# A decoder layer on one core: the merging of two attentions is spread over more steps, with hi and lo rows in one operand

## Chip, core and metric

The kernel runs on one core of a Trainium2 chip. The metric is device time in microseconds (us) of one execution. Three runs of the kernel before gave 892.7, 892.76 and 892.86 us; the median is 892.76.

The engines are named as the profile names them: PE multiplies matrices (PEld loads its stationary operand), DVE and ACT work element by element, POOL is a further such engine, SP issues most of the DMAs. Each engine takes its instructions in the order in which the program lists them.

## What is computed

One decoder layer of width 1024 over 512 tokens: a projection, two mixers side by side (dilated attention, and a state space model with a gated linear unit), their gated sum, a norm, and a gated feed-forward with a second norm. The change concerns the end of the attention, where the outputs of three dilation groups are merged by their softmax denominators:

```python
for g, (window, dilation) in enumerate(DILATION_GROUPS):   # (128,1), (512,4), (2048,16)
    o_g, lse_g = dilated_group_attention(q[:, :, g], k[:, :, g], v[:, :, g], window, dilation)
    outs.append(o_g)
    lses.append(lse_g)
wts = jax.nn.softmax(jnp.stack(lses, axis=0), axis=0)
attn = jnp.sum(wts[..., None] * jnp.stack(outs, axis=0), axis=0)
y_attn = attn.reshape(bsz, s, ATTN_WIDTH).astype(x.dtype) @ w_attn_br[layer]
...
glu = jax.nn.gelu(y_s).astype(x.dtype) @ w_glu[layer]
y_s = glu[..., :SSM_WIDTH] * jax.nn.sigmoid(glu[..., SSM_WIDTH:])
y_ssm = y_s @ w_ssm_br[layer]
```

## The kernel before

Every fp32 operand of a large product is held as two parts, hi and lo (`split`: ACT rounds the hi part, DVE subtracts to get the lo part), and a product is three matmuls, hi by hi, hi by lo and lo by hi (`mm3`, L186 to L188). A tile of 512 tokens by 128 channels is a chain of such triples into one PSUM bank. Weights come by DMA in units of 1 MB and are split likewise, one half at each `w.release()`: ACT writes `whi`, DVE writes `wlo`.

The order is written out by hand. The program is a list of steps, one PE tile or pair of tiles each, and `at_step(n, fn)` hangs smaller work into step n: a whole number runs in the middle of the step (`mid`, after half of the matmuls, or where a later loop calls `run_fill`), a number ending in .5 at its end. Steps 0 to 55 are the tiles of the first projection; 52 to 55 are gate tiles (`pg`). Steps 56 to 59 are the four tile pairs of the gated linear unit (GLU, banks `gl`, in a ring of four banks, so pair n+2 overwrites pair n). Its eviction is a tanh on ACT (`th`), a multiply on DVE, and a split into `gh` and `gl`. Steps 60 to 63 multiply its result by the state space branch's weights (banks `b`), steps 64 to 67 do the same for the attention's result (`ath`, `atl`).

The attention itself runs between these tiles. It is done in two kinds: kind 0, near, is the first dilation group; kind 1, far, is the other two together. Each unit of work has scores (PE, `s`), a masked maximum (DVE) and an exponential (ACT), transposes of the result into a bank (`t`, PE; there are two such banks, `turned`, taken in turn), a copy of that bank by ACT (`tv`), and the values (PE, `o`). Far attention's units are at steps 46 to 56.5; near attention is done by step 40.5. Each kind leaves its outputs in `oa` and two statistics per head and token in `st`: a shifted maximum and a sum.

The merge then needs, per head and token, the weight of each kind. Before the change:

- Step 56, after the matmuls of the first GLU pair and ahead of its eviction: `merge_stats` loads the selector `sel` (8 rows, one per head; it spreads a head's weight over its 64 channels), turns the statistics of both kinds with 16 transposes through the two `turned` banks (`stb`), copies them by DVE, takes the common maximum, and exponentiates on ACT.
- Step 57, ahead of the second pair's eviction: `merge_weights`, three operations of DVE and a reciprocal.
- Step 58, ahead of the third pair's eviction: `merge_split` makes hi and lo parts (`whl`) of the two weights, each of 8 rows, as four separate operands.
- Steps 59.5 to 62.5: `merge_pair`, for each pair of heads, spreads the weights by four matmuls (`wb`, two per kind, hi and lo added in PSUM) and scales and adds the two outputs on DVE; ACT and DVE split the sum.

In the profile the small helpers have one line for all callers: `split` is L179, L180, L182 and L183, `tt` is L302, `stt` is L299.

Of the kernel before, what the change touches and what calls it, by code (L numbers as in the profile page):

```python
# [10 lines left out]
F32 = mybir.dt.float32  # L11
# [3 lines left out]
ALU = mybir.AluOpType  # L15
# [39 lines left out]
def by_phase(z):  # L55
    return z.rearrange("p (r h c) -> p r h c", r=4, h=2)
# [96 lines left out]
def emit(ctx, tc, i, out):  # L153
# [48 lines left out]
    def big(n, name, dt=F32):  # L202
        return pa.tile([P, 2048], dt, tag=f"big{n}", name=name)
# [574 lines left out]

    merged = {}

    def merge_stats():
        sel = at.tile([8, NPAIR, P], F32, tag="sw", name="sel")
        sp.dma_start(sel, i["sel"])
        stt_ = big(1, "sts")
        sts = [[stt_[0:8, 512 * (2 * k + e) : 512 * (2 * k + e + 1)] for e in range(2)] for k in range(2)]
        for kind in range(2):
            for e in range(2):
                b = turned(f"stb{kind}{e}")
                for blk in range(4):
                    pe.transpose(b[0:8, 128 * blk : 128 * blk + 128], st[kind][:, e, blk, :], ident)  # L790
                if kind == 0:
                    dve.tensor_copy(by_phase(sts[kind][e]), as_phases(b[0:8]))
                else:
                    dve.tensor_copy(sts[kind][e], b[0:8])
        mg = at.tile([8, 512], F32, tag="sw", name="mg")
        tt(mg, sts[0][0], sts[1][0], ALU.min)
        for kind in range(2):
            tt(sts[kind][0], mg, sts[kind][0], ALU.subtract)
        for kind in range(2):
            act.activation(sts[kind][0], sts[kind][0], AF.Exp)  # L800
        merged.update(sel=sel, sts=sts)

    def merge_weights():
        sts = merged["sts"]
        zg = at.tile([8, 512], F32, tag="cq", name="zg")
        for kind in range(2):
            tt(sts[kind][1], sts[kind][0], sts[kind][1], ALU.mult)
        tt(zg, sts[0][1], sts[1][1], ALU.add)
        dve.reciprocal(zg, zg)
        merged["z"] = zg  # L810

    def merge_split():
        sts = merged["sts"]
        selr = at.tile([8, NPAIR, P], F32R, tag="tv", name="selr")
        dve.tensor_copy(selr, merged["sel"])
        hl = big(3, "whl", F32R)
        whl = [[hl[0:8, 512 * (2 * k + e) : 512 * (2 * k + e + 1)] for e in range(2)] for k in range(2)]
        for kind in range(2):
            tt(sts[kind][0], sts[kind][0], merged["z"], ALU.mult)
        for kind in range(2):  # L820
            act.copy(whl[kind][0], sts[kind][0])
        for kind in range(2):
            tt(whl[kind][1], sts[kind][0], whl[kind][0].bitcast(F32), ALU.subtract)
        merged.update(sel=selr, w=whl)
        for j, n in (("g1", "h"), (1, "l")):
            merged[n] = home(j, f"at{n}", F32R).rearrange("p (q t) -> p q t", q=4)

    def merge_pair(hp):
        wb = [turned(f"wb{hp}{k}") for k in range(2)]
        for kind in range(2):  # L830
            for e in range(2):
                pe.matmul(wb[kind], merged["sel"][:, hp, :], merged["w"][kind][e], start=(e == 0), stop=(e == 1))
# [130 lines left out]
    for n in range(4):  # L963
        ws = w.views[N_GLU + n]
        bs = []
        for e in range(2):
            b = glu(f"gl{n}{e}")
            co = slice(128 * e, 128 * e + 128)
            for k in range(4):
                mm3(b, (ws[0][:, k, co], ws[1][:, k, co]), (gluin["y"][0][:, k, :], gluin["y"][1][:, k, :]), k == 0, k == 3)  # L970
            bs.append(b)
        run_fill(N_GLU + n)
        th = at.tile([P, 512], F32, tag="sw", name=f"th{n}")
        act.activation(th, bs[1], AF.Tanh, scale=0.5)
# [232 lines left out]
def constants():  # L1207
# [18 lines left out]
    sel = np.zeros((8, NPAIR, P), f32)  # L1226
    for hp in range(NPAIR):
        for m in range(P):
            sel[2 * hp + m // 64, hp, m] = 1.0
    return {"rope": rope, "masks": masks, "sel": sel, "ident": np.eye(P, dtype=f32)}  # L1230


# [72 lines left out]
```

## Time and profile before

| what | value |
|---|---|
| median of three runs | 892.76 us |
| the profiled execution, whole | 892.44 us |
| its span in the trace | 890.7 us |
| steps 56 to 59, first GLU matmul to first matmul of step 60 | 390.65 to 419.03 us |
| steps 60 to 63, to the first matmul on `ath` | 419.03 to 447.33 us |
| granted TensorE clock, mean | 0.997 |

The page gives each engine's busy time. A timeline row gives start and duration in us, engine, line, operation and the tiles it writes and reads; `x8` means that eight neighbours are merged into a row; in brackets at its end stands how long the engine was idle before it, and what it waited for. Matmuls overlap in the trace, so two starts, not a duration, give PE's pace.

### The profile page before, as it was taken

The page shows a single profiled execution, that of the slowest core. Times are in us where ns is not written, and L with a number is a line of the kernel's source. Part 1 is how long each engine was busy: PE and PEld are TensorE (multiplying, and loading weights), DVE is VectorE, ACT ScalarE, POOL GpSimd, SP SyncE. Part 2 cuts the span into 40 slices and gives each one's busy share as a digit, 9 for nine tenths or more (in the row PEclk, how much of TensorE's full clock was granted, in tenths as well). Part 3 has the DMA queues.
Part 4 walks back from the last instruction along what each step waited for, and adds up shares of the span by engine and source line. Part 5 has one row for each costly group of instructions (what it writes and reads, how often), then busy time and mean ns, then how long its engine had stood idle before and what let it go on. Part 6 is the DMA issues. An engine that isn't in the chain of part 4 may idle for free.

```text
span 890.7 us, 11572 instructions
## 1 busy us (share of the span) xinstructions
PE 874.8 (98%) x4710; PEld 725.8 (81%) x4710; DVE 487.1 (55%) x929; ACT 292.2 (33%) x474; POOL 25.1 (3%) x26
## 2 busy tenths in 40 slices
PE   8999999999999999999999999999999999999996
PEld 5888888888878988876788898888888888888885
DVE  7887876665365464347876765333444444322237
ACT  5353521234442234544234233222222222211101
POOL 0000000000000000000000310000000000000004
PEclk9999999999999999999999999999999999999998
DMA  8843798062122222111225414222222222322203
GB/s 312 186 111 108 187 141 191 4 186 95 54 89 81 71 88 82 61 50 53 100 84 214 164 49 142 94 95 95 95 95 95 95 95 95 141 95 95 95 0 95
DMA packets 34789, 95.27 MB, mean 107 GB/s; under 512 B 11560, under 2 KB 21544, under 8 KB 25520
## 3 DMA queue, kind: packets, MB, share of 16 engines
q1 hardware_dynamic: 33152, 91.92, 33.6%
q10 hardware_dynamic: 1584, 2.61, 0.8%
q8 instruction: 37, 0.61, 0.3%
q14 instruction: 16, 0.13, 0.1%
HBM read 86.43 MB, written 4.69 MB: 102 GB/s over the span
## 4 chain that ended last, share of the span: by engine, by line
PE 49%; issue 40%; DVE 5%; DMA 3%; ACT 2%; POOL 2%; SPq 0%; DVEq 0%; POOLq 0%
PE pg L186 3%; PE pg L187 3%; PE pg L188 3%; PE pv L186 3%; PE pv L188 3%; PE pv L187 3%; PE pq L186 2%; PE pq L188 2%; PE pq L187 2%; PE pk L186 2%; PE s L733 2%; PE pk L188 2%; PE pk L187 2%; PE t L757 2%; PE b L186 2%
## 5 line engine op out<-in xcount | busy, mean ns | idle before, releaser
L180 DVE TENSOR_TENSOR wlo<-raw,whi 128x1024 fp32r<-128x1024 f32 x136 | 166.4, 1227 | 202.0 <-ACT whi L179 201.8
L179 ACT CAST whi<-raw 128x1024 fp32r<-128x1024 f32 x136 | 141.8, 1047 | 205.7 <-PE dn L188 74.8
L186 PE MATMUL fg<-hh,whi 128*128 128x512 f32 (+1 forms) x384 | 143.5, 374 | 0.0
L188 PE MATMUL fg<-hh,wlo 128*128 128x512 f32 (+1 forms) x384 | 143.4, 373 | 0.0
L187 PE MATMUL fg<-hl,whi 128*128 128x512 f32 (+1 forms) x384 | 143.4, 373 | 0.0
L187 PEld LDWEIGHTS fg<-hl,whi 128*128 128x128 f32 x384 | 72.3, 188 | 13.4
L188 PEld LDWEIGHTS fg<-hh,wlo 128*128 128x128 f32 x384 | 72.3, 188 | 13.3
L186 PEld LDWEIGHTS fg<-hh,whi 128*128 128x128 f32 x384 | 72.3, 188 | 13.3
L186 PE MATMUL dn<-whi,ff 128*128 128x512 f32 x168 | 66.0, 393 | 0.0
L188 PE MATMUL dn<-whi,ff 128*128 128x512 f32 x168 | 65.9, 392 | 0.0
L187 PE MATMUL dn<-wlo,ff 128*128 128x512 f32 x168 | 65.8, 392 | 0.0
L186 PE MATMUL pg<-x_hi,whi 128*128 128x512 f32 x128 | 50.6, 395 | 0.0
L188 PE MATMUL pg<-x_hi,wlo 128*128 128x512 f32 x128 | 49.9, 390 | 0.0
L187 PE MATMUL pg<-x_lo,whi 128*128 128x512 f32 x128 | 49.8, 389 | 0.0
L182 ACT ACTIVATE ff<-fth 128x512 fp32r<-128x512 f32 x22 | 13.9, 634 | 101.6 <-DVE fth L302 101.6
L745 ACT ACTIVATE pt<-pt,st 128x256 f32<-128x256 f32 (+1 forms) x64 | 31.0, 485 | 45.2 <-DVE st L743 45.2
L302 DVE TENSOR_TENSOR fth<-fth,fg 128x512 f32<-128x512 f32 x22 | 15.1, 688 | 55.8 <-PE fg L188 55.6
L186 PE MATMUL pq<-x_hi,whi 128*128 128x512 f32 x96 | 38.1, 397 | 0.0
L186 PE MATMUL pk<-x_hi,whi 128*128 128x512 f32 x96 | 38.0, 396 | 0.0
L188 PEld LDWEIGHTS dn<-whi,ff 128*128 128x128 f32 x168 | 31.5, 188 | 7.3
L188 PE MATMUL pq<-x_hi,wlo 128*128 128x512 f32 x96 | 37.4, 390 | 0.0
L188 PE MATMUL pk<-x_hi,wlo 128*128 128x512 f32 x96 | 37.4, 390 | 0.0
(236 smaller groups left out, 1592.0 us busy)
## 6 DMA issues: line engine op xcount, KB each, us to landing
raw<-in_w_in SPq DMA_DIRECT2D x27, 1024.0 KB, 5.1
raw<-in_w_gu SPq DMA_DIRECT2D x22, 1024.0 KB, 4.7
raw<-in_w_dn SPq DMA_DIRECT2D x11, 1024.0 KB, 4.7
raw<-in_w_br SPq DMA_DIRECT2D x4, 1024.0 KB, 4.8
raw<-in_w_out SPq DMA_DIRECT2D x4, 1024.0 KB, 4.7
cas<-ca SPq DMA_DIRECT2D x8, 256.0 KB, 7.8
tm<-kdr SPq DMA_DIRECT2D x16, 128.0 KB, 8.7
raw<-in_w_glu SPq DMA_DIRECT2D x2, 1024.0 KB, 4.7
```

What stands on the lines that cost most here:

```text
L179: act.copy(hi, src)
L180: dve.tensor_tensor(lo, src, hi.bitcast(F32), op=ALU.subtract)
L182: act.mul(hi, src, scale)
L186: pe.matmul(dst, a[0], b[0], start=first, stop=False)
L187: pe.matmul(dst, a[0], b[1], start=False, stop=False)
L188: pe.matmul(dst, a[1], b[0], start=False, stop=last)
L302: eng.tensor_tensor(o, a, b, op=op)
L733: pe.matmul(banks[hh][:, 256 * j + 128 * c : 256 * j + 128 * (c + nk)], z[0][rows, hp, qs], z[1][rows, hp, 128 * k0 : 128 * (k0 + nk)], st ...
L745: act.activation(pt[:, :n], pt[:, :n], AF.Exp, bias=mneg, scale=-1.0, accum_out=zsum)
L757: pe.transpose(tb[:, hh, cs], pts[hh][:, cs], ident)
```

## The change

Statistics are turned one kind at a time: the near ones in the middle of step 52, the far ones at the end of step 55. The further work of the merge is cut into smaller pieces, `merge_shift` (56.5), `merge_sum` (57.5), `merge_reciprocal` (58) and `merge_split` (59). In the GLU's loop `run_fill(N_GLU + n)` moves behind the eviction and the release of the weights. The pairs move from 59.5 + hp to 60 + hp, the middle of steps 60 to 63. Hi and lo rows of a weight become one operand of 40 rows, hi in rows 0 to 7, lo in rows 32 to 39, zeros between (filled by POOL), and the selector has its rows twice, so that one matmul per kind and pair does both. The small tiles of the merge now lie in the table `rope`, whose last reader is step 51, and in one scratch tile.

```diff
-    def merge_stats():
-        sel = at.tile([8, NPAIR, P], F32, tag="sw", name="sel")
-        sp.dma_start(sel, i["sel"])
...
-        for kind in range(2):
-            for e in range(2):
-                b = turned(f"stb{kind}{e}")
...
+    def merge_stats(kind):
+        if kind == 0:
+            merged["s"] = [[rope[0:8, e, :] for e in range(2)]]
+            sp.dma_start(rope[64:104, 0], i["sel"].rearrange("h p m -> h (p m)"))
+        else:
+            z = big(1, "sts")
+            merged["s"].append([z[0:8, 512 * e : 512 * (e + 1)] for e in range(2)])
+            merged["raw"] = z
+        for e in range(2):
+            b = turned(f"stb{kind}{e}")
+            for blk in range(4):
+                pe.transpose(b[0:8, 128 * blk : 128 * blk + 128], st[kind][:, e, blk, :], ident)
...
+    def merge_shift():
+        (m0, _), (m1, _) = merged["s"]
+        mg = merged["raw"][0:8, 1024:1536]
+        tt(mg, m0, m1, ALU.min)
+        for m in (m0, m1):
+            tt(m, mg, m, ALU.subtract)
+        for m in (m0, m1):
+            act.activation(m, m, AF.Exp)
+
+    def merge_sum():
+        (m0, z0), (m1, z1) = merged["s"]
+        merged["z"] = zg = merged["raw"][0:8, 1536:2048]
+        tt(z0, m0, z0, ALU.mult)
+        tt(z1, m1, z1, ALU.mult)
+        tt(zg, z0, z1, ALU.add)
+
+    def merge_reciprocal():
+        dve.reciprocal(merged["z"], merged["z"])
...
     def merge_split():
-        selr = at.tile([8, NPAIR, P], F32R, tag="tv", name="selr")
-        dve.tensor_copy(selr, merged["sel"])
+        sel = at.tile([40, NPAIR, P], F32R, tag="tv", name="selr")
         hl = big(3, "whl", F32R)
...
+        merged.update(sel=sel, w=[hl[0:40, 512 * k : 512 * (k + 1)] for k in range(2)])
+        act.copy(sel, rope[64:104, 0].rearrange("h (p m) -> h p m", p=NPAIR))
+        pool.memset(hl[0:40, 0:1024].bitcast(F32), 0.0)
+        for (m, _), w_ in zip(merged["s"], merged["w"]):
+            tt(m, m, merged["z"], ALU.mult)
+            act.copy(w_[0:8], m)
+            tt(w_[32:40], m, w_[0:8].bitcast(F32), ALU.subtract)
...
         for kind in range(2):
-            for e in range(2):
-                pe.matmul(wb[kind], merged["sel"][:, hp, :], merged["w"][kind][e], start=(e == 0), stop=(e == 1))
+            pe.matmul(wb[kind], merged["sel"][:, hp, :], merged["w"][kind], start=True, stop=True)
...
-    at_step(56, merge_stats)
-    at_step(57, merge_weights)
-    at_step(58, merge_split)
+    at_step(52, merge_stats, 0)
+    at_step(55.5, merge_stats, 1)
+    at_step(56.5, merge_shift)
+    at_step(57.5, merge_sum)
+    at_step(58, merge_reciprocal)
+    at_step(59, merge_split)
     for hp in range(NPAIR):
-        at_step(59.5 + hp, merge_pair, hp)
+        at_step(60 + hp, merge_pair, hp)
...
-        run_fill(N_GLU + n)
         th = at.tile([P, 512], F32, tag="sw", name=f"th{n}")
         act.activation(th, bs[1], AF.Tanh, scale=0.5)
         stt(th, th, 1.0, bs[0], ALU.add, ALU.mult)
         split(gh_[:, n, :], gl_[:, n, :], th, 0.5)
         w.release()
+        run_fill(N_GLU + n)
         run_fill(N_GLU + n + 0.5)
```

What the change does to the engines' order is seen at three places. First, PE in the middle of step 52, a gate tile (`pg`), as a difference; `stb` are the statistics' banks, `st` the near statistics:

```order
 L187 MATMUL pg_3256<-x_lo_83,whi_52_3088 128x512
 L188 MATMUL pg_3256<-x_hi_81,wlo_52_3089 128x512
+L794 MATMUL stb_3270<-ident,st_220 8x128 x4
+L794 MATMUL stb_3276<-ident,st_220 8x128 x4
 L186 MATMUL pg_3256<-x_hi_82,whi_52_3088 128x512
 L187 MATMUL pg_3256<-x_lo_84,whi_52_3088 128x512
```

Eight transposes now stand between the twelfth and the thirteenth matmul of that tile. The eight of the far kind stand in the same way behind the last attention transposes of step 55.5, ahead of the first GLU matmul.

Second, DVE around the evictions of the GLU, steps 57 to 59. Before (`th` is the eviction's multiply, `gl` its lo part, `wlo` a weight's lo part, `sts` the statistics, `zg` the sum):

```order
L302 TENSOR_TENSOR zg<-sts 8x512
L809 RECIPROCAL zg<-zg 8x512
L299 SCALAR_TENSOR_TENSOR th_3659<-th_3659,gl_3628 128x512
L183 SCALAR_TENSOR_TENSOR gl<-th_3659,gh 128x512
L180 TENSOR_TENSOR wlo_60_3665<-raw_3438,whi_60_3664 128x1024
L815 CAST selr<-sel 8x512
L302 TENSOR_TENSOR sts<-sts,zg 8x512 x2
L302 TENSOR_TENSOR whl<-sts,whl 8x512 x2
L299 SCALAR_TENSOR_TENSOR th_3705<-th_3705,gl_3668 128x512
L183 SCALAR_TENSOR_TENSOR gl<-th_3705,gh 128x512
L180 TENSOR_TENSOR wlo_61_3711<-raw_3438,whi_61_3710 128x1024
L299 SCALAR_TENSOR_TENSOR th_3742<-th_3742,gl_3716 128x512
```

And in the change, from step 58's eviction (`th_3690`) on; `rope` and `sts` hold the near and the far weights:

```order
L299 SCALAR_TENSOR_TENSOR th_3690<-th_3690,gl_3664 128x512
L183 SCALAR_TENSOR_TENSOR gl<-th_3690,gh 128x512
L180 TENSOR_TENSOR wlo_61_3696<-raw_3451,whi_61_3695 128x1024
L817 RECIPROCAL sts<-sts 8x512
L299 SCALAR_TENSOR_TENSOR th_3728<-th_3728,gl_3702 128x512
L183 SCALAR_TENSOR_TENSOR gl<-th_3728,gh 128x512
L180 TENSOR_TENSOR wlo_62_3734<-raw_3610,whi_62_3733 128x1024
L302 TENSOR_TENSOR rope<-rope,sts 8x512
L302 TENSOR_TENSOR whl<-rope,whl 8x512
L302 TENSOR_TENSOR sts<-sts 8x512
L302 TENSOR_TENSOR whl<-sts,whl 8x512
L302 TENSOR_TENSOR oa_3113<-oa_3113,wb_3768 128x512
```

The reciprocal moved from ahead of step 57's eviction to behind step 58's, and the four operations that make `whl` from ahead of step 58's to behind step 59's; they now alternate with ACT kind by kind.

Third, PE where the first pair of heads is spread. Before, between the last GLU matmul and step 60 (`b`):

```order
L188 MATMUL gl_3729<-yh,wlo_59_3614 128x512
L832 MATMUL wb_3751<-whl,selr 128x512 x2
L832 MATMUL wb_3752<-whl,selr 128x512 x2
L186 MATMUL b_3767<-gh,whi_60_3664 128x512
L187 MATMUL b_3767<-gl,whi_60_3664 128x512
```

And in the change, between the two halves of step 60:

```order
L187 MATMUL b_3751<-gl,whi_60_3657 128x512
L188 MATMUL b_3751<-gh,wlo_60_3658 128x512
L836 MATMUL wb_3767<-whl,selr 128x512
L836 MATMUL wb_3768<-whl,selr 128x512
L186 MATMUL b_3764<-gh,whi_60_3657 128x512
```

The matmuls on `whl` moved twelve matmuls later on PE, and there are two of them in place of four.

More of the change, by code (lines that the diff above doesn't have):

```diff
@@ L803, in merge_weights @@
[L803 to L810, printed above, removed]
+    def merge_stats(kind):
[10 more added lines that the diff above has]
+                pe.transpose(b[0:8, 128 * blk : 128 * blk + 128], st[kind][:, e, blk, :], ident)
+            if kind == 0:
+                dve.tensor_copy(by_phase(merged["s"][0][e]), as_phases(b[0:8]))
+            else:
+                dve.tensor_copy(merged["s"][1][e], b[0:8])
@@ L820, in merge_split @@
[L820 to L826, printed above, removed]
+        merged.update(sel=sel, w=[hl[0:40, 512 * k : 512 * (k + 1)] for k in range(2)])
+        act.copy(sel, rope[64:104, 0].rearrange("h (p m) -> h p m", p=NPAIR))
```

27 lines of the change are left out of this document (6 added, 21 removed).

## The prediction

> **What bounds the kernel now.** I read the page's busy line first, then the list of what PE waited for over the whole run, then the timeline from step 51 to step 64.
>
> ```profile
> PE 874.8 (98%) x4710; PEld 725.8 (81%) x4710; DVE 487.1 (55%) x929; ACT 292.2 (33%) x474; POOL 25.1 (3%) x26
> ...
> PE b L186 <- ACT gh L182: 1.2, 1, 1.2
> ...
> PE gl L186 <- DVE th L299: 0.8, 1, 0.8
> ...
> PE stb L790 <- DVE sts L792: 0.3, 1, 0.3
> PE b L187 <- DVE gl L183: 0.2, 1, 0.2
> ```
>
> PE is the bound: 874.8 of 890.7 us. Because it works nearly without a break, the time is the sum of what PE issues and of the moments when it can issue nothing; work of DVE and ACT counts only where PE's next instruction needs it. The four waits quoted (a wait's row: total, times, longest) all lie in or just behind the merge, so the change is priced by asking, place by place, when PE can issue its next instruction. PE's pace there:
>
> ```profile
> 426.21 0.39 PE L187 MATMUL b<-gl,whi 128*128 128x512 f32 x1
> 426.44 0.40 PE L188 MATMUL b<-gh,wlo 128*128 128x512 f32 x1
> 426.76 1.19 PE L832 MATMUL wb<-whl,selr 8*128 8x512 f32 x4
> 427.88 0.50 PE L186 MATMUL b<-gh,whi 128*128 128x512 f32 x1
> ```
>
> Columns are start, duration, engine, line, operation. Durations overlap; starts count. One 512-column matmul takes a slot of 0.23 us (426.21 to 426.44), and a change to another kind of operand takes 0.32 (426.44 to 426.76).
>
> **The change, part by part.** (1) *Half the spreading matmuls.* Each pair issues two of them, not four: four pairs by two by 0.23 is **-1.85 us**. The new operand has 40 rows, which the trace does not show; 8 rows (wb) and 128 rows (b) both take 0.23, so I take 0.23.
>
> (2) *Statistics leave the linear unit (GLU).*
>
> ```profile
> 396.08 0.40 PE L188 MATMUL gl<-yh,wlo 128*128 128x512 f32 x1
> 396.31 1.04 PE L790 MATMUL stb<-ident,st 128*8 128x128 f32 x8
> ...
> 398.81 1.09 PE L771 MATMUL o<-tv,v 128*64 128x128 f32 x16
> ```
>
> Sixteen transposes stand between step 56's GLU matmuls and the last attention values; 2.73 us pass from the last matmul to the values. Without them it is a mere change of operand, 0.32: **-2.4 us**. A transpose takes (1.04 - 0.27)/7 = 0.11 us, 0.27 being the length of one.
>
> (3) *Near statistics at step 52.* Eight transposes go between the halves of a gate tile. They write the two banks that the transposes of step 51.5 have just filled and that ACT empties:
>
> ```profile
> 359.92 0.39 PE L188 MATMUL pg<-x_hi,wlo 128*128 128x512 f32 x1
> 360.14 0.39 PE L186 MATMUL pg<-x_hi,whi 128*128 128x512 f32 x1
> ...
> 360.66 1.04 ACT L759 COPY tv<-t 128x512 f32<-128x512 f32 x2
> ```
>
> PE is at the middle of the tile at 360.14, but ACT, behind four exponentials, copies the two banks only from 360.66 to 361.70. The first four transposes start about 361.3, the second four at 361.76, and the tile goes on 0.44 + 0.1 later, at 362.3: **+2.2 us**, of which 1.2 is waiting and 1.0 the transposes themselves. Nothing later gets it back, since PE waits for nothing in steps 53 to 55. The two DVE copies fall into idle time and free the banks well before step 52.5. The DMA of the larger selector (40 rows, not 8) moves ahead of two weight loads on SP; its data is used 50 us later.
>
> (4) *Far statistics at step 55.5*, straight behind the last attention transposes, again into their two banks:
>
> ```profile
> 389.80 1.09 PE L757 MATMUL t<-ident,pt 128*128 128x128 f32 x8
> 390.55 1.07 ACT L759 COPY tv<-t 128x512 f32<-128x512 f32 x2
> 390.65 0.48 PE L186 MATMUL gl<-yh,whi 128*128 128x512 f32 x1
> ```
>
> The GLU starts at 390.65 now. Then the second four transposes must wait for the copy that ends at 391.62, and the GLU starts at 391.68 + 0.44 + 0.1 = 392.2: **+1.6 us**, 0.65 of it waiting.
>
> (5) *Merge behind the eviction.* One chain, from step 57 to the first pair of heads, carries the prices of three places:
>
> ```profile
> 405.30 0.39 PE L188 MATMUL gl<-yh,wlo 128*128 128x512 f32 x1
> 405.73 0.60 ACT L974 ACTIVATE th<-gl 128x512 f32<-128x512 f32 x1 [0.26 <-PE gl L188]
> 408.18 3.34 DVE L809 RECIPROCAL zg<-zg 8x512 f32<-8x512 f32 x1
> 410.90 0.40 PE L188 MATMUL gl<-yh,wlo 128*128 128x512 f32 x1
> 411.45 0.62 DVE L299 SCALAR_TENSOR_TENSOR th<-th,gl 128x512 f32<-128x512 f32 x1
> 412.10 0.63 ACT L182 ACTIVATE gh<-th 128x512 fp32r<-128x512 f32 x1 [5.77 <-DVE th L299]
> 412.12 0.50 PE L186 MATMUL gl<-yh,whi 128*128 128x512 f32 x1 [0.82 <-DVE th L299]
> 412.77 0.69 DVE L183 SCALAR_TENSOR_TENSOR gl<-th,gh 128x512 fp32r<-128x512 f32 x1 [0.70 <-ACT gh L182]
> 414.85 0.41 DVE L815 CAST selr<-sel 8x512 fp32r<-8x512 f32 x1
> 415.19 1.27 DVE L302 TENSOR_TENSOR sts<-sts,zg 8x512 f32<-8x512 f32 x2
> 415.89 1.22 ACT L821 CAST whl<-sts 8x512 fp32r<-8x512 f32 x2 [2.22 <-DVE sts L302]
> 416.54 1.28 DVE L302 TENSOR_TENSOR whl<-sts,whl 8x512 fp32r<-8x512 f32 x2
> 417.92 1.18 PE L832 MATMUL wb<-whl,selr 8*128 8x512 f32 x4
> ```
>
> Now the reciprocal stands ahead of step 57's eviction, whose bank step 59 needs: PE stops from 411.13 (410.90 + 0.23) to 412.12. With the eviction first, this goes: **-1.0 us**.
>
> What is late next? The reciprocal moves behind step 58's eviction, hence ahead of step 59's. Count from the start t = 0 of step 58's last matmul. Activation at 0.43 (405.30 to 405.73), multiply at 1.04, DVE free 3.40 later (411.45 to 414.85): reciprocal at 4.44. (Step 57, 5.6 earlier, frees DVE at -1.2 in the same way; merge_sum's three operations of 0.67 end at 0.85, in time.) It holds DVE for 3.27 (408.18 to 411.45), so step 59's multiply starts at 7.71; the hi half is done 1.28 later, at 8.99, the lo half at 9.72. PE finishes step 59 (24 slots) at 5.8 and nine matmuls of step 60 at 7.9, and needs the hi half there: it waits to 9.05, then to 9.8 for the lo half, 1.66 us in all. Before, the same place cost 1.87:
>
> ```profile
> 420.99 0.40 PE L188 MATMUL b<-gh,wlo 128*128 128x512 f32 x1
> 422.60 0.50 PE L186 MATMUL b<-gh,whi 128*128 128x512 f32 x1 [1.21 <-ACT gh L182]
> 423.32 0.50 PE L187 MATMUL b<-gl,whi 128*128 128x512 f32 x1 [0.23 <-DVE gl L183]
> ```
>
> (421.22 to 422.60, and 0.49 at the lo half.) So **-0.2 us**.
>
> Then comes the new wait. PE reaches the first spreading matmul, in the middle of step 60, at 10.4. But merge_split stands on DVE behind step 59's eviction and the weight split, so it starts at 7.71 + 3.40 = 11.11, and the two kinds go through DVE, ACT, DVE one after the other: multiply; ACT's cast 0.70 on, at 11.81; DVE's subtract at 12.46, done at 13.13. The second kind's multiply can start only at 13.07, its cast at 13.77, its subtract at 14.42, done at 15.09. With 0.10 for the release (417.82 to 417.92) PE issues the first spreading matmul at 13.2 and the second at 15.2, not 10.65: **+4.5 us**. Queued behind them on PE are the second half of step 60 and everything after; behind merge_split on DVE, pair 0. Steps 61 to 63 then run without a wait. DVE's period per pair
>
> ```profile
> 424.65 0.68 DVE L302 TENSOR_TENSOR oa<-oa,wb 128x512 f32<-128x512 f32 x1
> 430.80 0.68 DVE L302 TENSOR_TENSOR oa<-oa,wb 128x512 f32<-128x512 f32 x1
> ```
>
> is 6.15 us and fits into PE's 6.4 (26 slots and two changes, some restart), so pair 3 ends about a microsecond before step 64 needs it.
>
> The cast of the selector goes to ACT, idle there; cover gone, it costs 0.4. POOL's fill of 40x1024 is new to the trace. It may start when the last values are done, some 20 us before use, so I take 0. The other end is a slowed DVE: beside POOL's normalisation a weight split takes 1.48 us,
>
> ```profile
> 502.17 1.48 DVE L180 TENSOR_TENSOR wlo<-raw,whi 128x1024 fp32r<-128x1024 f32 x1 [1.16 <-ACT whi L179]
> ```
>
> not the 1.23 it takes elsewhere, and 0.25 would pass down the chain.
>
> **Sum:** -1.85 - 2.4 + 2.2 + 1.6 - 1.0 - 0.2 + 4.5 = +2.85 us. The profiled execution took 892.44 us (span 890.7), 0.3 below the median 892.76: 895.3 against the first, 895.6 against the second. I say **895.4 us**.
>
> **Rivals.** (a) *Slower still, by the clock.* The new wait is 2.8 us of idle PE, one matmul, and 1.7 us more.
>
> ```profile
> 881.67 0.28 PE L188 MATMUL dq<-whi,ff 128*128 128x256 f32 x1
> ...
> 885.00:885.20 0.20, 0.00 (x0) 0.00 (x0) 0.20 (x2) 0.00 (x0) 0.00 (x0) 1.00 1.02 225
> 885.40:885.60 0.20, 0.00 (x0) 0.00 (x0) 0.20 (x1) 0.00 (x0) 0.00 (x0) 0.50 0.16 41
> ```
>
> In these windows the last three columns are granted clock, DMA share and GB/s. Some 3.4 us after PE's last matmul (ended 881.95) the clock falls to 0.50. Neither idle piece is that long; together they are. If the one matmul does not hold the clock up, and half speed lasts as long as the fall took, 3.4 us of work do 1.7: 897.1 us. Chance 0.12. The Trainium skill, TensorE: Matmul & The Clock Gate, section "HAM oscillation — how this bites in real kernels", warns of idle gaps over about 3.4 us; the trace's end agrees in length, but no run here shows two shorter gaps with one matmul between them.
>
> (b) *Faster: the weights are there in time.* If merge_split were done when PE reaches the middle of step 60, the +4.5 falls away: 890.9 us, and less if (c) holds too. It decides at t = 10.4; the chain above misses it by almost 5 us, with each link from a row. For it: I may have misjudged what the first matmul waits for. Chance 0.11.
>
> (c) *No wait for the banks at 52 and 55.5*, if ACT had emptied them when the transposes come: 1.2 + 0.65 less, 893.5 us. Against it: ACT's copies are in the trace, behind named work, 0.5 us after PE would be there. Chance 0.12.
>
> (d) *The joined operand doesn't halve the matmuls' time*: +1.85, 897.2 us. Chance 0.03.
>
> **How the numbers follow.** The forecast keeps 0.62. A measurement of this kernel tells about 0.2%, 1.8 us, from no change. Faster is (b), 0.11; same is (c), 0.12; slower is the forecast with (a) and (d), 0.77. From 893.2 to 897.3 lie the forecast, (a), (c) and (d), 0.89 before I allow for errors inside each; (b) is left out.
>
> **What would show it.** Right: PE waits of about 2.8 and 1.8 us at wb for DVE's whl; stb transposes waiting on ACT's tv at steps 52 and 55.5; no wait of gl for th; a wait of b for gh of about 1.2. Wrong: no wait at wb (b), or a granted clock below 1.00 in the 4 us behind it (a).

## The result, and the profile after

The changed kernel takes 898.5 us, the median of 6 runs (897.65 to 902.15); the kernel before, run beside it, took 892.67 (6 runs, 892.43 to 892.86). The ratio is 1.0061, with a 95% interval of 1.0039 to 1.0082: slower, by more than the 895.4 us forecast and outside the range of 893.2 to 897.3. The profiled execution is the slowest of the six, 902.15 us with a span of 900.4.

To see where 9.7 us of that execution lie, the run is cut at four instructions that both kernels have: the first and the last `pk` matmul (both well ahead of the change), the first GLU matmul `gl`, and the first matmul `b` of the attention's result, behind the merge. The rows come from the view of one tile's instructions: shortest, median and longest duration in ns, then the start of the first and of the last one in us. The kernel before:

```profile
L186 PE MATMUL pk<-x_hi,whi x96: 389/389/501, 130.1 to 322.8; 128*128 128x512 f32 x96
L186 PE MATMUL gl<-yh,whi x32: 390/394/499, 390.7 to 417.1; 128*128 128x512 f32 x32
L186 PE MATMUL b<-ath,whi x32: 393/394/396, 447.3 to 468.9; 128*128 128x512 f32 x32
```

The changed kernel:

```profile
L186 PE MATMUL pk<-x_hi,whi x96: 389/389/774, 130.6 to 328.1; 128*128 128x512 f32 x96
L186 PE MATMUL gl<-yh,whi x32: 390/393/502, 399.4 to 422.4; 128*128 128x512 f32 x32
L186 PE MATMUL b<-ath,whi x32: 393/393/394, 457.3 to 478.6; 128*128 128x512 f32 x32
```

| Stretch, us | before | after | difference |
|---|---|---|---|
| start to the first `pk` | 130.1 | 130.6 | +0.5 |
| first to last `pk` (nothing changed here) | 192.7 | 197.5 | +4.8 |
| A: last `pk` to first `gl` (steps 52 and 55.5) | 67.9 | 71.3 | +3.4 |
| B: first `gl` to first `b` of the attention (GLU, merge) | 56.6 | 57.9 | +1.3 |
| C: from there to the end of the span | 443.4 | 443.1 | -0.3 |

The first lesson is in the second row: half of this execution's loss lies ahead of every instruction that the change touches. A and B are the change; together they cost 4.7 us, where the forecast had 2.85. A longest `pk` matmul of 774 ns, where 501 is the longest before, says in what way the untouched stretch grew: the clock of TensorE (PE) was lower in it.

The list of what PE waited for in the changed kernel (us in total, times, longest) has what the prediction named, and one row it did not:

```profile
PE wb L836 <- DVE whl L302: 4.1, 2, 2.8
PE yb L660 <- DMA h<-hst: 1.7, 2, 1.2
...
PE stb L794 <- ACT tv L759: 1.3, 2, 1.0
PE b L186 <- ACT gh L182: 1.1, 1, 1.1
```

The wait of `gl` for `th` (0.8 before) is gone; `stb` waits for ACT's `tv`; `wb` waits for `whl`. The row of `yb`, 0.2 before, is the new one: a DMA of the state space model's state `h`, which the change does not touch.

The timeline of steps 52 and 55.5 in the changed kernel (start, duration, engine, line, operation, and in brackets how long the engine stood idle ahead of it and what ended that):

```profile
365.23 0.39 PE L188 MATMUL pg<-x_hi,wlo 128*128 128x512 f32 x1
366.59 1.08 PE L794 MATMUL stb<-ident,st 128*8 128x128 f32 x8 [0.97 <-ACT tv L759]
367.43 0.48 PE L186 MATMUL pg<-x_hi,whi 128*128 128x512 f32 x1
...
397.20 1.09 PE L757 MATMUL t<-ident,pt 128*128 128x128 f32 x8
398.58 1.09 PE L794 MATMUL stb<-ident,st 128*8 128x128 f32 x8 [0.29 <-ACT tv L759]
399.43 0.48 PE L186 MATMUL gl<-yh,whi 128*128 128x512 f32 x1
```

Without the turns the tile of step 52 would have gone on at 365.46, a slot of 0.23 behind 365.23; it goes on at 367.43, 2.0 us later. At 55.5, `t` to `gl` takes 2.23 us, where it took 0.85 (389.80 to 390.65): 1.4 us more. Together that is the 3.4 us of A.

Step 60 of the changed kernel, PE alone:

```profile
426.45 0.50 PE L186 MATMUL b<-gh,whi 128*128 128x512 f32 x1 [1.14 <-ACT gh L182]
427.17 0.50 PE L187 MATMUL b<-gl,whi 128*128 128x512 f32 x1 [0.23 <-DVE gl L183]
427.51 0.40 PE L188 MATMUL b<-gh,wlo 128*128 128x512 f32 x1
430.65 0.79 PE L836 MATMUL wb<-whl,selr 40*128 40x512 f32 x1 [2.75 <-DVE whl L302]
432.82 0.76 PE L836 MATMUL wb<-whl,selr 40*128 40x512 f32 x1 [1.37 <-DVE whl L302]
433.51 0.79 PE L186 MATMUL b<-gh,whi 128*128 128x512 f32 x1
434.10 0.63 PE L187 MATMUL b<-gl,whi 128*128 128x512 f32 x1
434.53 0.63 PE L188 MATMUL b<-gh,wlo 128*128 128x512 f32 x1
...
437.31 0.39 PE L186 MATMUL b<-gh,whi 128*128 128x512 f32 x1
437.54 0.39 PE L187 MATMUL b<-gl,whi 128*128 128x512 f32 x1
```

The two waits of the forecast are there (2.8 and 1.8 were foreseen). Behind them the matmuls start 0.43 us apart (434.10 to 434.53), and only from 437 on 0.23 apart again. The windows of the same stretch say why. Their columns are the stretch, its length, the busy time of PE, PEld, DVE, ACT and POOL with the number of instructions, and then the granted clock, the DMA share and GB/s:

```profile
426.00:430.00 4.00, 1.23 (x3) 0.48 (x3) 2.60 (x4) 2.56 (x4) 0.00 (x0) 1.00 0.00 0
430.00:434.00 4.00, 1.97 (x3) 1.06 (x4) 2.34 (x4) 0.62 (x1) 0.00 (x0) 0.53 0.00 0
434.00:438.00 4.00, 4.00 (x12) 3.07 (x12) 3.28 (x5) 0.62 (x1) 0.00 (x0) 0.62 0.00 0
438.00:442.00 4.00, 4.00 (x17) 2.78 (x16) 2.28 (x4) 1.05 (x1) 0.00 (x0) 1.00 0.23 39
```

The clock was granted at 0.53 and 0.62 of full speed in the 8 us from 430 to 438; read in windows of 0.2 us it is at 0.50 from 430.2 to 437.0 and at 1.00 on both sides. PE is busy all the time from 434 to 438 and still does 12 matmuls where the next window has 17: a busy share cannot show this loss, the count beside it can. This was rival (a) of the prediction.

Far ahead of the change, around the matmuls into `yb`, the same column of the same kernel reads:

```profile
150.00:154.00 4.00, 4.00 (x23) 4.00 (x22) 1.16 (x2) 0.00 (x0) 0.00 (x0) 0.54 0.42 127
154.00:158.00 4.00, 4.00 (x13) 3.27 (x13) 1.80 (x3) 1.23 (x2) 0.00 (x0) 0.61 0.35 145
```

The kernel before had 1.00 in both windows.

### The profile page after: what moved, and what is told of

It is laid out like the page before. It is cut to its first block, busy times and chain, and to the rows that moved or that the text cites. A ratio compares the mean times of both kernels' runs of the same rounds, so it can differ in the third digit from the quotient of the medians.

```text
span 900.4 us, 11559 instructions
## 1 busy us (share of the span) xinstructions
PE 880.4 (98%) x4702; PEld 730.0 (81%) x4702; DVE 486.8 (54%) x928; ACT 292.9 (33%) x475; POOL 26.1 (3%) x27
## 4 chain that ended last, share of the span: by engine, by line
PE 49%; issue 39%; DVE 4%; DMA 3%; ACT 2%; POOL 2%; SPq 0%; DVEq 0%; POOLq 0%; ACTq 0%
PE pg L186 3%; PE pg L188 3%; PE pg L187 3%; PE pv L186 3%; PE pv L188 3%; PE pv L187 3%; PE pq L186 2%; PE pq L188 2%; PE pq L187 2%; PE pk L186 2%; PE pk L187 2%; PE pk L188 2%; PE b L186 2%; PE s L733 2%; PE b L187 2%
## 5 line engine op out<-in xcount | busy, mean ns | idle before, releaser
L182 ACT ACTIVATE ff<-fth 128x512 fp32r<-128x512 f32 x22 | 13.9, 634 | 101.6 <-DVE fth L302 101.6
L302 DVE TENSOR_TENSOR fth<-fth,fg 128x512 f32<-128x512 f32 x22 | 15.1, 688 | 55.8 <-PE fg L188 55.6
L187 PE MATMUL pk<-x_lo,whi 128*128 128x512 f32 x96 | 37.9, 395 | 0.0
```

Of the source, the lines that this page charges most:

```text
L182: act.mul(hi, src, scale)
L187: pe.matmul(dst, a[0], b[1], start=False, stop=False)
L302: eng.tensor_tensor(o, a, b, op=op)
```

## The experiments

Three questions were open. Is the loss near 150 us part of the change? Is it really the waits at `wb` that lower the clock in step 60, and which of them? And are the terms of the sum what the prediction said, each by itself?

The expectations call PE TensorE, DVE VectorE and ACT ScalarE. Since single runs of most kernels turned out to scatter by several us, each experiment is read twice: by its times beside those of the kernel before on the same chip, and by the stretches A and B of its profile, which leave out what happened earlier. C is 442.9 to 443.5 us in all fourteen profiles.

| Kernel | first to last `pk` | A | B | median us (all runs) | before, same chip: median (all runs) |
|---|---|---|---|---|---|
| before | 192.7 | 67.9 | 56.6 | 892.67 (892.43 to 892.86) | |
| after | 197.5 | 71.3 | 57.9 | 898.5 (897.65 to 902.15) | 892.67 (892.43 to 892.86) |
| e1 held clock | 192.9 | 71.4 | 55.8 | 895.81 (894.5 to 901.84) | 894.0 (891.74 to 899.03) |
| e2 no weights | 197.7 | 71.3 | 51.5 | 894.04 (891.05 to 897.2) | 894.0 (891.74 to 899.03) |
| e3 joined only | 199.4 | 67.9 | 55.5 | 893.99 (892.74 to 898.37) | 894.0 (891.74 to 899.03) |
| e4 40-row input | 192.3 | 67.9 | 56.7 | 893.24 (892.27 to 897.44) | 894.0 (891.74 to 899.03) |
| e5 late yb | 192.2 | 71.4 | 58.3 | 897.6 (896.98 to 897.95) | 893.47 (892.03 to 899.98) |
| e6 first wait filled | 192.3 | 71.3 | 55.9 | 896.41 (894.99 to 904.11) | 893.47 (892.03 to 899.98) |
| e7 free banks | 193.4 | 69.7 | 57.8 | 896.3 (895.17 to 898.9) | 893.47 (892.03 to 899.98) |
| e8 rearranged | 192.3 | 69.6 | 50.5 | 888.02 (887.42 to 890.39) | 893.47 (892.03 to 899.98) |
| e9 before, late yb | 192.3 | 67.9 | 56.7 | 892.06 (891.77 to 893.2) | 892.85 (892.25 to 898.27) |
| e10 second wait filled | 192.9 | 71.3 | 57.3 | 899.2 (897.48 to 900.35) | 892.85 (892.25 to 898.27) |
| e11 before, eviction first | 192.3 | 67.8 | 67.1 | 901.37 (900.13 to 904.49) | 892.85 (892.25 to 898.27) |
| e12 one gap left | 193.1 | 71.4 | 58.8 | 899.62 (897.53 to 904.95) | 893.88 (892.4 to 899.27) |

### The loss near 150 us: e4, e5, e9

e4 is the kernel before with the 40-row selector in DRAM, of which it loads the 8 rows that it did before:

```diff
-    sel = np.zeros((8, NPAIR, P), f32)
+    sel = np.zeros((40, NPAIR, P), f32)
...
-        sp.dma_start(sel, i["sel"])
+        sp.dma_start(sel, i["sel"][0:8])
```

> The kernel before, whose selection matrix has 40 rows in DRAM, of which it loads the same 8. Theory C (the loss near 150 us comes with the layout of the inputs in DRAM): runs scatter from 892.7 up to 897, with TensorE waiting over 1 us for h at the matmuls into yb in the profiled run. Theory D (it has nothing to do with the input): 892.7 within 0.3, all runs alike.

Its ten runs go from 892.27 to 897.44, but the 31 runs of the unchanged kernel before, on the same chip, go from 891.74 to 899.03. So neither theory holds as it was put: the scatter is there with and without the larger input, and with and without the change. That the kernel before had shown six equal runs beside the changed one was chance or the chip.

e5 moves the output of the state space model (`ssm_out`; the expectation calls it a part of the linear unit), the matmuls into `yb` that wait for `h`, one step later in the changed kernel; e9 does the same in the kernel before:

```diff
-        at_step(22.5 + 0.5 * q, ssm_out, q)
+        at_step(23.5 + 0.5 * q, ssm_out, q)
-    at_step(24.5, turn_y)
+    at_step(25.5, turn_y)
```

> The changed kernel with the four pieces ssm_out of the linear unit (matmuls into yb) and turn_y one step later (23.5 to 25, 25.5). The profiles so far: where the matmuls into yb waited 1.7 us or more for h (the changed kernel, e2, e3), the clock fell to 0.54 to 0.66 around 150 us and the stretch from the first pk to the last took 197.5 to 199.4 us; where they waited under 0.5 us (before, e1, e4) it took 192.3 to 192.9. Theory: the upper half of the runs comes from that wait, which no kernel of this study changes. Then here no matmul into yb waits for h, that stretch is 192 to 193, and the runs lie together within about 2 us of 897.5. Rival: the scatter comes from elsewhere, for instance the start: runs up to 902 again.

> The kernel before with ssm_out and turn_y one step later, as in e5. If the scatter of the kernel before (892.0 to 900.0 in the last 19 runs) is the wait of the matmuls into yb for h and the clock behind it, all runs lie between 891.7 and 893.5. If it is the start of the kernel or something else, they reach 896 again.

Both came as the first theory said. In e5 and e9 no row of the list of PE's waits names `yb`, the clock around it is 1.00 (e5):

```profile
150.00:154.00 4.00, 4.00 (x26) 3.53 (x25) 2.69 (x5) 1.04 (x1) 0.00 (x0) 1.00 0.35 88
154.00:158.00 4.00, 4.00 (x29) 3.72 (x29) 3.80 (x6) 0.60 (x1) 0.00 (x0) 1.00 0.43 178
```

and the stretch of the `pk` tiles is 192.2 and 192.3 us. The changed kernel's runs then lie between 896.98 and 897.95 (4 runs), those of the kernel before between 891.77 and 893.2 (10 runs), while the unrepaired kernel before beside them reached 899.98 and 898.27. Most of the scatter upwards belongs to the wait for `h`, not to the change. A smaller part lies earlier still: in the profiles of e1, e8 and e12 the clock is at 0.50 for 3.4 us from 12.4, 12.7 and 13.2 us on, and the first `pk` starts at 132.5 to 133.0 us, in place of 130.1 to 130.9 in the other eleven. With the wait for `h` gone from both kernels, the change costs 897.6 - 892.06 = 5.5 us (two chips); by A and B of these two profiles it is (71.4 + 58.3) - (67.9 + 56.7) = 5.1 us.

### The clock in step 60: e1, e6, e10, e12

e1 fills both waits with spare matmuls that write a bank nobody reads:

```diff
+        hold = outs("hold") if hp == 0 else None
         for kind in range(2):
+            if hp == 0:
+                for _ in range((12, 6)[kind]):
+                    pe.matmul(hold, w.views[N_BR][0][:, 0, 0:128], gh_[:, 0, :], start=True, stop=True)
             pe.matmul(wb[kind], merged["sel"][:, hp, :], merged["w"][kind], start=True, stop=True)
```

> The changed kernel with twelve spare 512-column matmuls on TensorE ahead of the first wb and six between the two of pair 0, in the two waits for whl (2.75 and 1.37 us); they write a bank that nobody reads. Theory A (the clock falls because TensorE idles twice): the 512-column matmuls behind wb keep their 0.23 us spacing, the granted clock in the 10 us behind is 0.95 or more, and the time is about 895.5 us where nothing else is lost, against 897.7 for the fastest runs of the changed kernel. Theory B (the clock falls for another reason, such as power drawn by the step): 0.66 again, and 897.7 or more. Either way the wait for whl itself stays, now filled. What is lost near 150 us, ahead of the change, is not touched and may add up to 4 us to a run.

The windows of e1 behind the two waits:

```profile
428.00:432.00 4.00, 3.98 (x15) 2.45 (x14) 2.69 (x5) 0.62 (x1) 0.00 (x0) 1.00 0.00 0
432.00:436.00 4.00, 4.00 (x19) 3.21 (x19) 3.28 (x6) 1.58 (x2) 0.00 (x0) 1.00 0.01 4
```

The clock stays at 1.00, B falls from 57.9 to 55.8, and the median is 895.81 (ratio to before 1.0034, interval 1.0016 to 1.0053). By B, eighteen added matmuls make the kernel 2.1 us faster, because they stand where PE has to wait anyway. Theory A holds; power drawn by the step is out, since e1 does more work in it, not less. B of e1 is also the place to test the rest of the forecast without the clock, and it gives 55.8 - 56.6 = -0.8 us, against -0.95 in the prediction's terms.

e6 and e10 leave one of the two waits open; against e1, the edit of e6 stands first, that of e10 second.

```diff
-            if hp == 0:
-                for _ in range((12, 6)[kind]):
+            if hp == 0 and kind == 0:
+                for _ in range(12):
...
-            if hp == 0:
-                for _ in range((12, 6)[kind]):
+            if hp == 0 and kind == 1:
+                for _ in range(6):
```

> The changed kernel with the twelve spare matmuls in the first wait for whl alone, so that TensorE idles 1.37 us once in step 60. If one idle piece of 1.37 us is enough for the fall: spacing 0.43 behind it and the stretch from the first gl to the first b of the attention 57.5 to 58 us as in the changed kernel (57.9). If it takes the two pieces together: spacing 0.23 throughout and 55.8 as in the run with both filled.

> The changed kernel with six spare matmuls in the second wait for whl alone: TensorE idles once, 2.75 us, in step 60. If the fall of the clock needs both idle pieces together: spacing 0.23 throughout, first gl to first b of the attention 55.8 us as in e1 and e6. If one idle piece of this length is enough: spacing 0.43 for some 6 us and 57.5 to 58.3 as in the changed kernel and e5.

In e6 PE idles 1.58 us ahead of the second `wb`, the next matmuls keep their pace, and B is 55.9: here a piece of that length did nothing. In e10 it idles 2.75 us ahead of the first, the clock is at 0.50 from 426.8 to 430.2 us, and B is 57.3 (57.5 to 58.3 had been expected): so it does not take the two together, as the prediction had assumed for (a). But 1.13 and 0.22 us of waiting for `gh` and `gl` lie close ahead of the 2.75, so e12, which is e10 with one more edit, fills those as well:

```diff
+    early = outs("early")
...
             for k in range(4):
+                if n == 0 and c == 0 and k == 3:
+                    for _ in range(6):
+                        pe.matmul(early, ws[0][:, 0, co], gh_[:, 0, :], start=True, stop=True)
                 mm3(b, (ws[0][:, k, co], ws[1][:, k, co]), (src[0][:, k, :], src[1][:, k, :]), k == 0, k == 3)
```

> The kernel of e10 with six more spare matmuls where b waits for gh and gl (1.13 and 0.22 us) in step 60, so that the 2.75 us ahead of the first wb is the only idle piece there. If that one piece lowers the clock by itself: spacing 0.43 behind it and first gl to first b of the attention 57.3 us as in e10. If the idle pieces within some 5 us add up: spacing 0.23 and 55.8 as in e1 and e6.

Step 60 of e12:

```profile
425.52 0.39 PE L188 MATMUL b<-gh,wlo 128*128 128x512 f32 x1
428.67 0.50 PE L840 MATMUL wb<-whl,selr 40*128 40x512 f32 x1 [2.75 <-DVE whl L302]
429.09 2.47 PE L839 MATMUL hold<-gh,whi 128*128 128x512 f32 x6
431.49 0.79 PE L840 MATMUL wb<-whl,selr 40*128 40x512 f32 x1
...
435.36 0.63 PE L187 MATMUL b<-gl,whi 128*128 128x512 f32 x1
435.79 0.63 PE L188 MATMUL b<-gh,wlo 128*128 128x512 f32 x1
```

The six spare matmuls take 2.47 us, where they took 1.63 in e1, and the tile behind them runs at a spacing of 0.43 until 436.2. One idle piece of 2.75 us is enough to lower the clock. (B of 58.8 is more than the price of the fall, since the spare matmuls ran at half speed ahead of the second `wb`.)

The length of the piece is not the whole of it, though. The clock stays at 0.50 for 6.8 us in the changed kernel, e5, e7, e12 and at both falls of e11, for 3.4 us in e10 and for 10.2 us near 150 us in e3, all multiples of 3.41 us; and the two falls of e11, at 400.74 and 428.04, are eight times 3.41 us apart. So in these traces the granted clock changes only at the ends of steps of 3.41 us, counted through the whole run. Cut into such steps, e10 reads

```profile
423.40:426.81 3.41, 0.66 (x3) 0.25 (x2) 2.64 (x4) 0.86 (x2) 0.00 (x0) 1.00 0.00 0
426.81:430.22 3.41, 3.41 (x8) 2.01 (x7) 0.84 (x2) 0.62 (x1) 0.00 (x0) 0.50 0.00 0
430.22:433.63 3.41, 3.41 (x15) 2.74 (x15) 2.51 (x4) 0.69 (x2) 0.00 (x0) 1.00 0.00 0
```

and e12

```profile
426.25:429.67 3.42, 1.00 (x4) 0.67 (x5) 2.30 (x4) 0.93 (x2) 0.00 (x0) 1.00 0.00 0
429.67:433.08 3.41, 3.41 (x8) 2.04 (x7) 1.44 (x3) 0.30 (x1) 0.00 (x0) 0.50 0.00 0
433.08:436.49 3.41, 3.41 (x9) 2.64 (x9) 2.69 (x4) 0.62 (x1) 0.00 (x0) 0.50 0.00 0
436.49:439.90 3.41, 3.41 (x15) 2.49 (x14) 2.13 (x3) 1.05 (x1) 0.00 (x0) 1.00 0.02 5
```

In all fourteen profiles (the fall behind the kernel's last matmuls left out) the step ahead of a fall is one that PE filled only in part: it was busy for 0.12 to 1.16 us of 3.41 at the waits in step 60 and in e11, 0.87 to 1.41 near the start, 1.48 to 2.15 amid the matmuls into `yb`. Steps with 1.85 (before, 8.10 to 11.52) or 1.98 (before, 421.12 to 424.53) were not followed by one, so a step that is idle for half or more is a fair reading, with the 2.15 (e2) as the exception. In e6 the 1.58 us lie across the end of a step at 426.88 and leave PE 2.56 us busy ahead of it and 2.69 behind, so what 1.58 us inside one step would do is not shown. Why the clock came back after one step in e10 and after two in e12 is open.

The Trainium skill, TensorE: Matmul & The Clock Gate, section "HAM oscillation — how this bites in real kernels", gives about 3.4 us as the idle time to stay under. Here 2.75 us is too long, so the measurement sets the bound lower. The same page, in Part 1 on the clock gate, describes a window of about 3.4 us that runs freely. The steps of these traces agree with that, and so do the onsets: the fall comes 0.4 us ahead of the end of the 2.75 us in the changed kernel, 0.5 us behind it in e10 and 1.0 us behind it in e12.

### The terms one by one: e2, e3, e7, e11

e2 takes the wait away at its source: `whl` is a constant.

```diff
-        pool.memset(hl[0:40, 0:1024].bitcast(F32), 0.0)
-        for (m, _), w_ in zip(merged["s"], merged["w"]):
-            tt(m, m, merged["z"], ALU.mult)
-            act.copy(w_[0:8], m)
-            tt(w_[32:40], m, w_[0:8].bitcast(F32), ALU.subtract)
+        pool.memset(hl[0:40, 0:1024].bitcast(F32), 0.25)
```

> The changed kernel with whl filled by one constant at step 59; the two products with the reciprocal, their two copies on ScalarE and their two subtractions are left out. Theory A (the wait of wb for whl in step 60 is the dear part, 4.1 us plus 2 us of slow clock behind it): 891.0 to 892.0 us, no wait at wb for whl, clock 1.00 through step 60. Theory B (the turns of the statistics at steps 52 and 55.5 carry most of the loss): 895 us or more. Whatever is lost near 150 us comes on top of either.

B falls to 51.5 us. Of the 6.4 us to the changed kernel's 57.9, e1 puts 2.1 (57.9 to 55.8) on the clock; the other 4.3 are the wait itself, which the prediction had at 4.5. By A and B the kernel would be 1.7 us faster than before. Its times (ratio 1.0001, 0.9977 to 1.0025) show no such thing under the scatter, and its median of 894.04 misses the 891.0 to 892.0 of theory A; its profile has the loss near 150 us too. Its fastest run, 891.05, is 0.7 below the fastest of before.

e3 is the kernel before with the joined operand alone:

```diff
-        whl = [[hl[0:8, 512 * (2 * k + e) : 512 * (2 * k + e + 1)] for e in range(2)] for k in range(2)]
+        pool.memset(hl[0:40, 0:1024].bitcast(F32), 0.0)
+        whl = [[hl[32 * e : 32 * e + 8, 512 * k : 512 * (k + 1)] for e in range(2)] for k in range(2)]
...
-            for e in range(2):
-                pe.matmul(wb[kind], merged["sel"][:, hp, :], merged["w"][kind][e], start=(e == 0), stop=(e == 1))
+            pe.matmul(wb[kind], merged["sel"][:, hp, :], merged["w"][kind], start=True, stop=True)
```

> The kernel before with the joined 40-row operand alone: two spreading matmuls per pair in place of four, at the steps where they stood before. By the sum of the prediction: 8 matmuls less, -1.85 us, 890.8 us. Rival: the 40-row matmul is no faster per pair, 892.7. For the loss near 150 us: if it comes with the larger constant of the input (40 rows in place of 8), runs of this kernel scatter upwards by up to 4 us as those of the changed kernel did; if it comes with the moved instructions, they don't.

B is 55.5, 1.1 us less than before, not 1.85. The matmuls are halved at the expected pace; but the first pair stood in front of a wait, and that wait has grown:

```profile
424.79 0.72 PE L832 MATMUL wb<-whl,selr 40*128 40x512 f32 x2
429.65 0.50 PE L186 MATMUL b<-gh,whi 128*128 128x512 f32 x1 [1.76 <-ACT gh L182]
```

It was 1.21 us before. What PE saves ahead of a wait for another engine, it waits. In the times nothing is to be seen (ratio 1.0002, 0.9980 to 1.0023).

e7 turns the statistics into other banks, so that they need not wait for ACT's copies:

```diff
-            b = turned(f"stb{kind}{e}")
+            b = (dense, scores)[kind](f"stb{kind}{e}")
```

> The changed kernel with the statistics turned into other PSUM banks: those of the dense tiles at step 52, those of the scores at 55.5, in place of the two that ScalarE is still copying from. By the prediction's terms 3 and 4 the waits there are 0.97 and 0.29 us of the stretch from the last pk to the first gl, which was 67.9 us before and 71.3 after: 70.1 here, and the time 1.2 us under that of the changed kernel. Rival: the next dense tile then waits for the copies to VectorE, and the stretch stays 71.3 or grows.

A falls from 71.3 to 69.7 and no `stb` is in the list of PE's waits; its median is 896.3, 1.3 under e5's 897.6 (same chip), though e7 lacks e5's repair near 150 us. The waits for the banks were real and worth 1.6 us, somewhat more than the 1.26 idle that their rows show. The 1.8 us that A keeps over before are what sixteen transposes take at the prediction's 0.11 us each.

e11 is e9 with nothing but the eviction put ahead of the merge's pieces:

```diff
-        run_fill(N_GLU + n)
         th = at.tile([P, 512], F32, tag="sw", name=f"th{n}")
...
         w.release()
+        run_fill(N_GLU + n)
         run_fill(N_GLU + n + 0.5)
```

> The kernel of e9 with the eviction of the linear unit ahead of the merge's pieces, the statistics left at step 56. The prediction's term 5 gave this part alone -1.0 us, by the wait of gl for th that goes (TensorE 411.13 to 412.12): 891.4 against 892.4 of e9, if it stands by itself. Rival: it only pays because the statistics have left step 56; here their copies queue on VectorE behind th, gl and wlo, the third turn waits some 4 us for its bank, and the kernel is about 3 us slower than e9, 895.4.

It is slower than e9 by 901.37 - 892.06 = 9.3 us, three times what the rival gave. The list of PE's waits in e11:

```profile
PE stb L790 <- DVE sts L792: 4.0, 1, 4.0
PE wb L832 <- ACT whl L821: 3.5, 1, 3.5
```

The first wait is the rival's: the third turn finds its bank held, because DVE does `th`, `gl` and `wlo` first. The second was not foreseen: the chain of the weights, now behind each eviction, is not done at step 59.5. And both lower the clock (0.66 between 400 and 410 us, 0.76 between 430 and 440). So the order that the change gives the eviction does not pay while the statistics stay at step 56; the -1.0 us of term 5 cannot be had alone.

### Put together: e8

e8 keeps the change's parts, moves the chain of the weights one step earlier (VectorE has room there), gives the turns their free banks and the output of the linear unit its later step. Pairs 0 and 1 spread their weights at step 59.5, in the time in which `b` has to wait for `gh` and `gl`.

```diff
-    at_step(56.5, merge_shift)
-    at_step(57.5, merge_sum)
-    at_step(58, merge_reciprocal)
-    at_step(59, merge_split)
+    at_step(55.5, merge_shift)
+    at_step(56, merge_sum)
+    at_step(56, merge_reciprocal)
+    at_step(57, merge_split)
     for hp in range(NPAIR):
-        at_step(60 + hp, merge_pair, hp)
+        at_step((59.5, 59.5, 60.5, 61.5)[hp], merge_pair, hp)
...
-        wb = [turned(f"wb{hp}{k}") for k in range(2)]
+        wb = [(turned(f"wb{hp}{k}") if hp % 2 == 0 else bank((4, 7)[k], f"wb{hp}{k}")) for k in range(2)]
```

> The changed kernel put together anew: ssm_out a step later as in e5, the free banks of e7, shift at 55.5, sum and reciprocal at 56, split at 57 (each behind the eviction), pairs 0 and 1 at 59.5 with banks of their own, 2 at 60.5, 3 at 61.5. If each wait measured so far is what it seems: last pk to first gl 70.1, first gl to first b of the attention about 50.5 (51.5 in e2, whose spreading matmuls had nothing to wait for, less four of them in the 1.4 us that b waits for gh and gl), the rest 443.3: 4 us under the kernel before in its undisturbed runs, 888 to 889. Rival: VectorE, given the chain earlier, delays the evictions of the linear unit and gl waits for its banks: 891 or more.

It takes 888.02 us (6 runs, 887.42 to 890.39), against 893.47 for the kernel before on the same chip: ratio 0.9946, interval 0.9930 to 0.9962. It beats both kernels. In its profile the last subtraction into `whl` starts at 416.56 and PE is at the first `wb` at 418.18:

```profile
416.56 0.68 DVE L302 TENSOR_TENSOR whl<-sts,whl 8x512 fp32r<-8x512 f32 x1 [0.68 <-ACT whl L827]
...
418.18 1.18 PE L836 MATMUL wb<-whl,selr 40*128 40x512 f32 x4
422.13 0.50 PE L186 MATMUL b<-gh,whi 128*128 128x512 f32 x1 [0.49 <-ACT gh L182]
```

In the changed kernel the same subtraction started at 431.99, and relative to the first `gl` that is 32.6 us against 22.2 here. `wb` waits for nothing, the wait of `b` for `gh` has shrunk from 1.14 to 0.49, and A and B are 69.6 and 50.5, as expected (70.1 and about 50.5). Compared with e9, which has the same repair near 150 us, the gain is 4.0 us (two chips), or 4.5 by A and B.

## Why the prediction was wrong

The sign and the mechanisms were right, and the sum of the terms came close. It failed in what it made of one of them: the wait was counted as time alone, the clock behind it was put at nothing in the sum, and it was left to a rival with a chance of 0.12.

- **Terms 3 and 4, the turns at steps 52 and 55.5** (+2.2 and +1.6). Measured 2.0 and 1.4, as waits for the engine and at the places that were named; A grew by 3.4. e7 showed that the waits for the banks are a real part of it. Rival (c) is out.
- **Term 1, half the matmuls** (-1.85). As a pace it held; rival (d) is out. Alone it is worth 1.1 us (e3), because the first pair's share goes into the wait for `gh`.
- **Terms 2 and 5 and the wait at step 60** (-2.4, -1.0, -0.2). The transposes left the GLU, `gl` no longer waits for `th`, and `b` waits 1.14 for `gh`, as foreseen. None was measured alone, and e11 showed that term 5 cannot be. Terms 2 and 5 together can be read from the profile: from the first `gl` to the first matmul of step 60 it took 28.4 us before (390.65 to 419.03) and takes 23.6 in the changed kernel (399.43 to 423.06); 1.2 of the 4.8 us are the four spreading matmuls that left this stretch (0.23 from one matmul to the next, where 417.59 to 419.03 was 1.44), and 3.6 remain, against 3.4 foreseen.
- **The new wait of `wb` for `whl`** (+4.5). Two pieces, 2.75 and 1.37 us, at the place named, behind the chain named; taking it away is worth 4.3 (e2). Rival (b), the weights in time, is out for this kernel, and e8 shows what it would have been worth.
- **All of it together** was to be +2.85. Without the clock it is 3.4 - 0.8 = +2.6 us (A, and B of e1).
- **The step that failed** is the weighing of rival (a). The prediction said "Neither idle piece is that long; together they are", took the fall at the kernel's end, 3.4 us behind PE's last matmul, as the length that it needs, and gave (a) 0.12. In fact one piece of 2.75 us is enough (e12), since it left PE busy for only 1.00 us of one step of 3.41 us; the single piece of 1.58 us in e6 did not lower it. The clock fell in the profiles of the changed kernel, of e5 and of e7, in the same step of the program, and in all four runs of e5 its mean is 0.992 or 0.993, where the ten of e9, the kernel before with the same repair, have 0.995 or more; the price of 1.7 us put on (a) was about right: 2.1 (after against e1) to 2.5 (e5 against e1). Its 897.1 us is 0.5 below the 897.6 of e5, the changed kernel without the loss near 150 us.
- **What no step covered** is the scatter near 150 us. The kernel before's three runs lay within 0.2 us and its profile showed a wait of 0.2 us for `h`; from that the range was built as if everything upstream were fixed. The repair (e5 against after) lowers the median by 0.9 us, and no run is above 898. This is not what put the time outside the range: its upper end is 897.3, the median of e5 is 897.6, and even the fastest run of the changed kernel took 897.65.

## What to carry to other kernels

A wait that a change adds to the engine that bounds the kernel has two prices: its length, and the slow clock behind it; where that engine is PE, price the second wherever about half of a step of 3.41 us or more would be idle (here a single piece of 2.75 us), and look at the count of matmuls in a window, not at its busy share. When a producer's chain is late, try moving the chain's start; moving only its consumer later was not tried here. In e8 the same parts went from 5 us slower to 4 us faster, of which the earlier start of the weights and of the first pairs carries most (B from 58.3 in e5 to 50.5). And before a difference is explained, cut both runs at instructions that the change does not touch: half of the profiled loss lay in front of it.

## What the hardware did that was not expected

- The granted clock falls to 0.50 after a single idle piece of 2.75 us (e12: from 429.7 to 436.5 us). It changes only at the ends of steps of 3.41 us, and stays down for one (e10), two (the changed kernel, e2, e5, e7, e11, e12) or three of them (e3). In the changed kernel, where it is two, this costs 2.1 us (after against e1) to 2.5 (e5 against e1).
- Amid the narrow matmuls into `yb` (64 columns) waits of 1.23 and 0.42 us (after), 1.38 and 0.43 (e2) or 1.93 (e3) were followed by a clock of 0.50 for 6.8, 6.8 and 10.2 us, and the stretch from the first to the last `pk` grew by 5 to 7 us; waits of 0.34 and 0.42 us (e7) were not. In the step of 3.41 us ahead of the fall PE was busy for 1.76, 2.15 and 1.48 us. The 2.15 of e2 is more than the 1.85 and 1.98 that were not followed by a fall elsewhere; why was not tried.
- The DMA of `h` lands after 12.1 us in the median in one run and 13.9 or 14.4 in others (before, after, e3), under the same program upstream; why is open. Most of the spread of the kernel before, 892 to 900 us, goes with the wait for it, and is gone when the consumer comes one step later.
